# A conditioned decoder layer on one core: where the gate chunk's partial sums are added in the opening, and what orders the conditioning passes in the softmax

## The chip, the core and the metric

The kernel runs on one core of a Trainium2 chip. The core has a matrix engine (TensorE, PE in the profile, with its weight loads shown apart as PEld), a vector engine (VectorE, DVE), a scalar engine (ScalarE, ACT), a general engine (GpSimd, POOL) and an engine that mostly issues transfers (SyncE, SP). The metric is the device time of one execution in microseconds (us), as the median of several runs.

## What is computed

One layer: a SwiGLU feed-forward network, a mixing part with retention and windowed attention side by side, a second SwiGLU network, and a last norm. Scale, shift and gate of each part come from a product of a conditioning vector with a large matrix `w_ada`. Everything is float32. The core of it:

```python
c_act = jax.nn.silu(c)
mod = (c_act @ w_ada[l] + b_ada[l]).reshape(b, N_MOD, D_MODEL)
h = modulate(rms_norm(x, norm_ffn1[l]), mod[:, 0], mod[:, 1])
x = x + 0.5 * mod[:, 2][:, None, :] * swiglu(h, w_ffn1_gu[l], w_ffn1_down[l])
h = modulate(rms_norm(x, norm_mix[l]), mod[:, 3], mod[:, 4])
x = x + mod[:, 5][:, None, :] * token_mixing(h, w_in[l], ...)
h = modulate(rms_norm(x, norm_ffn2[l]), mod[:, 6], mod[:, 7])
x = x + 0.5 * mod[:, 8][:, None, :] * swiglu(h, w_ffn2_gu[l], w_ffn2_down[l])
```

with `swiglu(h) = (silu(gate) * up) @ w_down`, where gate and up are the two halves of `h @ w_gu`. There are 256 tokens (two halves of 128), the model width is 2048, the feed-forward width 5632.

## The kernel before

**Products.** Weights come from memory in pieces of 1 MB (four blocks of 128 rows by 512 columns) into one of four raw buffers (`load`, L365). `split` (L389, L391) makes two numbers of each weight: ACT casts it to a rounded `wh`, DVE subtracts to get the rest, `wl`. `products` (L374) then issues, for each block of rows, three products for each of the two token halves, so one split (two blocks) gives twelve matmuls of 512 columns. There are three pairs of `wh`/`wl` buffers. Sums stay in PSUM; the pool for them has four banks, and a chunk of 512 columns takes two, one for each token half.

**Who sets the order.** SP's instructions stay in the order in which the program writes them. The instructions of the other engines are ordered ahead of time by a list scheduler: each instruction may go as soon as its inputs and a buffer are free, and of those that may go the earliest in the program goes first. `tc.issue_after(x)` adds a rule that what is written inside comes behind `x` on the same engine. `low[-1]` is the latest subtraction for a `wl`, `cast[-1]` the latest cast. Some stages are ordered wholly by hand; the two that the change touches are not.

**The opening.** The first network's up product needs h, whose columns become ready as `w_ada` is worked through, so its first 16 chunks (eight pairs of a gate chunk, even, and an up chunk, odd) are computed in four groups of rows. After each group but the last, a chunk's sums are moved from the banks to `part_of(n)`, its parts in SBUF (`to_parts`). In the last group (rows 9 to 15, seven blocks, 42 matmuls a chunk) the chunks are visited in order 0 to 15. Nothing happens with the gate chunk's banks at the end of its own visit; after the up chunk's visit `swiglu_up` adds the parts to both (L720 for the gate, into a scratch tile of the pool `t512`, which has five; L721 for the up chunk, into the parts), applies Silu on ACT (L724), multiplies (L725) and hands the result on to be turned. After chunk 15 comes `ffn_up`, which computes the chunks that are left, whole.

**Conditioning.** `w_ada` is read row by row, a row being 2048 columns of 128 partitions (1 MB), and DVE multiplies and sums it with the conditioning vector in four passes of 512 columns (`ada_pass`, L222). From the opening's last group on this runs beside the products: `set_pace` starts a generator, `conditioning`, and `tick`, called after each set of products, advances it at a given rate, one pass a step. It asks for a row `pace["ahead"]` passes before the first use (L282, on SP). Each pass stands under `issue_after`: the first eight of a generator behind an operation handed to it, the others behind `low[-1]`.

In the mixing part the rows first lie in the raw buffers that the weights also use, two passes ahead; the rate is 0.95 of a pass for a set of products until the softmax starts, 0.25 (`RATE_SOFT`) during it, and 0.95 again after it (`RATE_AFTER`). Seven steps after that `rows_beside` moves the rows to a tile of their own, `rows_x`. The softmax runs in quads of heads beside the products: scores on PE (L1386), scale and mask (L1394), maxima (L1406), exponentials on ACT (L1415), scaling (L1422), split into planes on ACT (L1436), two transposes by transfer on SP (L1445), joining on DVE (L1457), and the product with the values (L1470).

Of the kernel before, what the change touches and what calls it, by code (L numbers as in the profile page):

```python
# [77 lines left out]
def layer_kernel(  # L78
# [23 lines left out]
    nc = tc.nc  # L102
# [106 lines left out]
    AQ = 4  # L209
# [7 lines left out]
    def ada_pass(k, w, sums, q, passes=AQ, first=0):  # L217

        n = D // passes
        at = slice(q * n, (q + 1) * n)  # L220
        here = w[:, (q - first) * n : (q + 1 - first) * n]
        nc.vector.tensor_tensor_reduce(  # L222
            out=here,
            in0=here,
            in1=cact[:, at],
            scale=1.0,
            scalar=0.0,
            op0=ALU.mult,
            op1=ALU.add,
            accum_out=sums[:, k, q : q + 1],  # L230
        )

    def ada_sums():
        return two.tile([P, KD, AQ], F32, tag="sums", name=nm("sums"))
# [33 lines left out]
    def conditioning(outputs, place, behind):  # L268


        tiles = [(m, k) for m, _, _ in outputs for k in range(KD)]
        held = {}
        step = asked = 0

        def ask(at):

            (m, k), q = tiles[at // AQ], at % AQ
            w = place()
            n = min(w.shape[1] * AQ // D, AQ - q)
            w = w[:, : n * D // AQ]  # L280
            c0 = q * D // AQ
            nc.sync.dma_start(  # L282
                w, w_ada[(m * KD + k) * P : (m * KD + k + 1) * P, c0 : c0 + n * D // AQ]
            )
            for i in range(n):
                held[at + i] = (w, q)
            return n

        for m, gain, row in outputs:
            sums = own_sums.pop() if own_sums else ada_sums()  # L290
            for k in range(KD):
                for q in range(AQ):
                    while asked <= step + pace["ahead"] and asked < AQ * len(tiles):
                        asked += ask(asked)
                    w, first = held.pop(step)
                    early_on = behind is not None and step < 2 * AQ
                    with tc.issue_after(behind.ins if early_on else low[-1]):
                        ada_pass(k, w, sums, q, first=first)
                    step += 1
                    if k == KD - 1 and q == AQ - 1:  # L300
                        ada_end(m, slice(0, KD), sums, gain)
                        if row is not None:
                            gate_out(m, row)
                    yield
# [16 lines left out]


    pace = {"steps": iter(()), "rate": 0.0, "due": 0.0, "behind": None}

    def set_pace(outputs, halves, place, ahead):
        assert next(pace["steps"], None) is None
        pace["steps"] = conditioning(outputs, place, pace["behind"])
        pace["rate"] = len(outputs) * KD * AQ / halves
        pace["due"] = 0.0
        pace["ahead"] = ahead  # L330
# [64 lines left out]
    cast, low, newest = [], [], []  # L395
# [314 lines left out]
    def swiglu_up(banks_g, banks_u, tiles, ci, parts=None, by_dma=False, behind=None):  # L710

        k0 = ci * KB
        dest = tiles[k0 // KD].rearrange("p (k s) -> p k s", s=S)
        kk = k0 % KD
        work = []
        for t in range(NT):
            s = t512()
            g, u = banks_g[t], banks_u[t]
            if parts is not None:
                nc.vector.tensor_add(s, g, parts[0][t])  # L720
                nc.vector.tensor_add(parts[1][t], u, parts[1][t])  # L721
                g, u = s, parts[1][t]
            with nullcontext() if behind is None else tc.issue_after(behind):
                nc.scalar.activation(s, g, AF.Silu)  # L724
            nc.vector.tensor_mul(s, s, u)  # L725
            if by_dma:
                work.append(turn_by_dma(dest[:, kk : kk + KB, t * P : (t + 1) * P], s))
                continue
            transpose_to(
                dest[:, kk : kk + KB, t * P : (t + 1) * P],  # L730
                lambda j: s[:, j * P : (j + 1) * P],
                KB,
            )
        if work:
            turns.append(later(work))
# [248 lines left out]
    behind = [[back.tile([P, CH], F32, tag="back", name=nm("back")) for _ in range(NT)] for _ in range(2)]  # L984

    def part_of(n):
        if n < 2:
            return behind[n]
        if n >= 14:
            return [beside[n - 14][:, t, :] for t in range(NT)]  # L990
        at = ((n - 2) % 4) * NT * CH
        return [part[(n - 2) // 4][:, at + t * CH : at + (t + 1) * CH] for t in range(NT)]
# [4 lines left out]
    def place(m, k):  # L997
        if k < 1:
            rows_of[m, k] = raw_row()
        else:  # L1000
            ring.reverse()
            rows_of[m, k] = ring[0]
        ada_load(m, k, rows_of[m, k], 2 if k < 2 else 1)
# [95 lines left out]
    banks, moved, unlinted, fresh, added = {}, set(), set(), set(), set()  # L1099
# [20 lines left out]
    with tc.manual_schedule(engines=ORDERED):  # L1120
# [14 lines left out]
        v, q = small(NT, "rvar"), small(NT, "rq2")  # L1135
# [118 lines left out]
    for g, ks in enumerate(groups):  # L1254
        final = g == len(groups) - 1
        by_vector = chunks[1::3] if g == 1 else ()
        if final:
            row_ring.append(two_rows(rows_home))
            set_pace(ROWS_FFN1, 192, place_row, 0)
        order = chunks if (len(groups) - g) % 2 else chunks[::-1]  # L1260
        coming = iter(()) if final else group(groups[g + 1], 1 if g == 0 else 2)
        due = 0 if final else 2 * len(groups[g + 1])
        stay = () if final else order[-2:]
        for i, n in enumerate(order):
            if g == 0 and n in firsts:
                continue
            visit(n, ks, n not in stay, final, final or (g == len(groups) - 2 and n in stay))
            if g:
                after = [(m, ks) for m in order[i + 1 : i + 2]]
                if not after and not final:  # L1270
                    after = [(n, groups[g + 1])]
                for m, ms in after:
                    ready(m, ms)
                    if m not in banks and not final:
                        open_banks(m, not (g == len(groups) - 2 and m in stay))
            if final:
                turn_step()
            last = len(order) - 2
            if g == 0:
                by = [min(due, -(-j * due // 12)) for j in (i - 2, i - 1)]  # L1280
                by = by[1] - by[0]
            else:
                by = (i + 1) * due // last - i * due // last if i < last else i == last
            for _ in range(by + (g == 0 and i == last)):
                next(coming, None)
            if g == 0:
                for m in {2: firsts[:1], 3: (order[2], firsts[1])}.get(i, order[i - 1 : i]):
                    if m not in stay:
                        to_parts(m)
                if i == 3:  # L1290
                    columns_rest()
                if i == 5:
                    roots_in_rows()
            if n in stay or g == 0:
                continue
            if not final:
                to_parts(n)
            elif n % 2:
                swiglu_up(
                    banks.pop(n - 1),  # L1300
                    banks.pop(n),
                    tiles,
                    n // 2,
                    (part_of(n - 1), part_of(n)),
                    n // 2 < 6,
                    cast[-1],
                )
# [15 lines left out]
    RATE_SOFT, RATE_AFTER = 0.25, 0.95  # L1323
    row_ring.clear()
    set_pace([(7, 2, None), (6, None, None), (5, None, 1.0)], 192 / 0.95, place_row, 2)

    def rows_beside():

        for _ in range(7):
            yield  # L1330
        row_ring.append(two_rows(one.tile([P, 2 * D], F32, tag="x", name="rows_x")))
        pace["ahead"] = 0

    def in_chunk(c0):
        return gemm(held, wi, [c0])[0]
# [9 lines left out]
    b = head  # L1345
# [14 lines left out]
    b = gemm(held, wi, [O_SV], ahead=ahead)[0]  # L1360
# [139 lines left out]
    for ci in range(4):  # L1500
        b = in_chunk(O_SQ + ci * CH)
        work = []
        for t in range(NT):
            u = t512()
# [14 lines left out]
    for a, off in ((0, O_RQ), (1, O_RK)):  # L1519
        for ci in range(2):  # L1520
            b = in_chunk(off + ci * CH)
            work = []
            for t in range(NT):
                u = t512()
# [71 lines left out]
    for ci in range(4):  # L1596
        b = in_chunk(O_RV + ci * CH)
# [14 lines left out]
    first = gates(0)  # L1612
# [3 lines left out]
    for ci in range(4):  # L1616
        b = in_chunk(O_RG + ci * CH)
        work = []
        for t in range(NT):
            u = t512()  # L1620
# [9 lines left out]
    for p in range(2):  # L1630
        sg = first if p == 0 else gates(p)
        c0s = [(2 * p + i) * CH for i in range(2)]
        for g, a, w in ((1, a_swa, w_swa_branch), (0, a_ret, w_ret_branch)):
            assert g == 1 or not turns
            banks = gemm(a, w[0], c0s)
# [150 lines left out]
```

## Time and profile before

| what | us |
|---|---|
| median of 3 runs | 2357.78 (2356.67 to 2358.15) |
| the profiled execution | 2356.72 |
| its span, first to last instruction | 2354.9 |
| PE busy | 2334.3 |
| DVE busy | 1684.4 |
| ACT busy | 1361.9 |
| the opening's last group | about 222 to 374.5 |
| the mixing part's products, as far as the softmax runs beside them | about 860 to 1105 |

The profiled execution is one of the program's executions; its trace is what the timeline, the waits and the chain are read from. A row of the timeline gives the start, the length, the engine, the line, the operation, output and inputs, the count of merged instructions and, in brackets, how long the engine was idle before and what ended that. A matmul is recorded with a modelled end, so consecutive ones overlap in the record; the time between starts is the better measure.

### The profile page before, as it was taken

How to read it: one execution, taken by the hardware profiler on the slowest of the kernel's cores; microseconds unless marked ns; L12 is line 12 of the kernel's file. 1: busy time of each engine (PE TensorE's matmuls, PEld its weight loads, DVE VectorE, ACT ScalarE, POOL GpSimd, SP SyncE). 2: the span in 40 equal slices, each digit the busy share in tenths (PEclk: the TensorE clock that was granted, in tenths of full speed). 3: DMA queues.
4: the chain of work that ended last, by engine and by line, in shares of the span. 5: the costliest groups of instructions: out<-in, count | busy, mean ns of one | idle time of the engine just before them, and what ended most of it. 6: DMA issues, size and time to landing. Idle time of an engine off the chain costs nothing.

```text
span 2354.9 us, 28573 instructions
## 1 busy us (share of the span) xinstructions
PE 2334.3 (99%) x10443; PEld 1917.9 (81%) x10443; DVE 1684.4 (72%) x2610; ACT 1361.9 (58%) x1889; POOL 19.9 (1%) x28
## 2 busy tenths in 40 slices
PE   8999999999999999999999999999999999999998
PEld 5888888888888887778888888888888888888887
DVE  7788887778877668876777876776555555555656
ACT  6776665455556567674556564466455454455544
POOL 0000000000000000000000000000000000000000
PEclk9999999999999999999999999999999999999999
DMA  9989999999875878877789888764777777776553
GB/s 367 341 344 390 312 326 345 307 294 321 285 269 217 275 265 243 243 216 268 282 266 312 286 301 284 276 223 177 236 243 249 248 239 259 242 240 201 193 197 125
DMA packets 205726, 630.37 MB, mean 268 GB/s; under 512 B 114641, under 2 KB 116433, under 8 KB 149265
## 3 DMA queue, kind: packets, MB, share of 16 engines
q1 hardware_dynamic: 203090, 617.54, 77.0%
q0 software_dynamic: 1600, 9.83, 1.1%
q8 instruction: 81, 1.33, 0.2%
q10 hardware_dynamic: 896, 1.19, 0.1%
q14 instruction: 59, 0.48, 0.1%
HBM read 598.60 MB, written 4.22 MB: 256 GB/s over the span
## 4 chain that ended last, share of the span: by engine, by line
PE 61%; DVE 1%; issue 0%; ACT 0%; DVEq 0%
PE pa L374 59%; PE ps L1470 0%; PE pd L1386 0%; PE ps L374 0%; DVE wl L391 0%; DVE soft L1457 0%; PE pd L1555 0%; PE pd L1568 0%; PE pd L1570 0%; PE pd L1569 0%; PE ps L1386 0%; PE ps L910 0%; DVE soft L1422 0%; PE pd L1558 0%; PE pd L910 0%
## 5 line engine op out<-in xcount | busy, mean ns | idle before, releaser
L391 DVE TENSOR_TENSOR wl<-raw,wh 128x1024 fp32r<-128x1024 f32 (+1 forms) x808 | 968.9, 1203 | 551.1 <-ACT wh L389 490.2
L389 ACT CAST wh<-raw 128x1024 fp32r<-128x1024 f32 (+1 forms) x808 | 833.1, 1037 | 829.5 <-PE pa L374 751.8
L374 PE MATMUL pa<-wh,hh 128*128 128x512 f32 x2184 | 598.1, 391 | 2.7 <-DVE a L721 1.3
L374 PE MATMUL pa<-wh,hl 128*128 128x512 f32 x2184 | 598.0, 390 | 0.0
L374 PE MATMUL pa<-wl,hh 128*128 128x512 f32 x2184 | 588.9, 389 | 0.9 <-DVE wl L391 0.9
L374 PEld LDWEIGHTS pa<-wh,hh 128*128 128x128 f32 x2184 | 407.6, 188 | 91.1 <-ACT wh L389 2.3
L374 PEld LDWEIGHTS pa<-wl,hh 128*128 128x128 f32 x2184 | 409.6, 188 | 87.5 <-DVE wl L391 1.8
L374 PEld LDWEIGHTS pa<-wh,hl 128*128 128x128 f32 x2184 | 409.7, 188 | 86.3 <-issue 0.8
L374 PE MATMUL pa<-wh,a 128*128 128x512 f32 x1824 | 452.1, 389 | 0.0
L374 PEld LDWEIGHTS pa<-wh,a 128*128 128x128 f32 x1824 | 341.6, 188 | 70.6
L222 DVE CUSTOM_DVE_ANT_0 slot<-slot,cact 128x512 f32<-128x512 f32 (+2 forms) x310 | 246.0, 803 | 6.0 <-DMA slot<-in_w_ada_dram 5.9
L374 PE MATMUL pa<-wl,a 128*128 128x512 f32 x912 | 245.1, 389 | 0.0
L374 PEld LDWEIGHTS pa<-wl,a 128*128 128x128 f32 x912 | 171.0, 188 | 35.4
L565 ACT COPY slot<-back 128x512 uint16<-128x512 uint16 x148 | 98.8, 767 | 0.0
L424 ACT CAST a<-slot 128x512 fp32r<-128x512 f32 x114 | 70.6, 620 | 32.8 <-PE pa L374 29.1
L222 DVE CUSTOM_DVE_ANT_0 rows_x<-rows_x,cact 128x512 f32<-128x512 f32 x124 | 84.9, 685 | 0.0
L425 DVE TENSOR_TENSOR a<-slot,a 128x512 fp32r<-128x512 f32 x114 | 78.1, 687 | 1.4 <-ACT a L424 1.2
L549 ACT COPY flat<-t 128x512 uint16<-128x512 uint16 x136 | 76.7, 618 | 2.6 <-DVE t L1543 1.6
L222 DVE CUSTOM_DVE_ANT_0 raw<-raw,cact 128x512 f32<-128x512 f32 (+1 forms) x72 | 51.0, 715 | 0.0
L1244 ACT COPY slot<-pa 128x512 f32<-128x512 f32 x64 | 34.7, 591 | 22.6 <-PE pa L374 22.5
L374 PE MATMUL pa<-wh,home 128*128 128x512 f32 x160 | 39.5, 389 | 0.0
L222 DVE DVE_READ_ACCUMULATOR2_ANT sums<- 128x1 f32 x442 | 36.7, 83 | 0.0
(234 smaller groups left out, 1090.4 us busy)
## 6 DMA issues: line engine op xcount, KB each, us to landing
raw<-in_w_ffn_gu_dram SPq DMA_DIRECT2D x144, 1024.0 KB, 5.7
raw<-in_w_in_dram SPq DMA_DIRECT2D x104, 1024.0 KB, 5.4
raw<-in_w_ffn_down_dram SPq DMA_DIRECT2D x88, 1024.0 KB, 5.1
slot<-in_w_ada_dram SPq DMA_DIRECT2D x132, 512.0 KB, 6.0
rows_x<-in_w_ada_dram SPq DMA_DIRECT2D x62, 512.0 KB, 6.0
slot<-in_w_ada_dram SPq DMA_DIRECT2D x28, 1024.0 KB, 7.3
raw<-in_w_ffn_gu_dram SPq DMA_DIRECT2D x32, 768.0 KB, 6.1
raw<-in_w_ada_dram SPq DMA_DIRECT2D x17, 1024.0 KB, 5.6
```

Of the source, the lines that this page charges most:

```text
L222: nc.vector.tensor_tensor_reduce(out=here, in0=here, in1=cact[:, at], scale=1.0, scalar=0.0, op0=ALU.mult, op1=ALU.add, accum_out=sums[:, ...
L374: product = nc.tensor.matmul(banks[t], act[:, j, t * P : (t + 1) * P], weights[:, j, :], start=starts and i == 0 and j == 0, stop=ends and ...
L389: cast.append(nc.scalar.copy(hi, src).ins)
L391: low.append(nc.vector.tensor_sub(lo, src, hi.bitcast(F32)).ins)
L424: nc.scalar.copy(hi, v)
L425: nc.vector.tensor_sub(lo, v, hi.bitcast(F32))
L549: nc.scalar.copy(planes[:, i, :], words(src)[:, :, i])
L565: nc.scalar.copy(into[:, :, :, i], held["turned"][:, i])
L1244: nc.scalar.copy(p, b)
```

## The change

In the opening's last group a gate chunk's sums are added to its parts, in place, at the end of its own visit, and `swiglu_up` then reads the gate from the parts. And a switch, `pace["one_by_one"]`, is on at first, is turned off as the mixing part's conditioning is set up, and on again when its rows move to `rows_x`; while it is off, passes after the first eight stand under no `issue_after`.

```diff
@@ conditioning
-                    early_on = behind is not None and step < 2 * AQ
-                    with tc.issue_after(behind.ins if early_on else low[-1]):
+                    first_ones = behind is not None and step < 2 * AQ
+                    if first_ones or pace["one_by_one"]:
+                        with tc.issue_after(behind.ins if first_ones else low[-1]):
+                            ada_pass(k, w, sums, q, first=first)
+                    else:
                         ada_pass(k, w, sums, q, first=first)
@@ beside the first pace
+    pace["one_by_one"] = True
@@ swiglu_up
             if parts is not None:
-                nc.vector.tensor_add(s, g, parts[0][t])
                 nc.vector.tensor_add(parts[1][t], u, parts[1][t])
-                g, u = s, parts[1][t]
+                g, u = parts[0][t], parts[1][t]
@@ the opening's loop over chunks
             if not final:
                 to_parts(n)
-            elif n % 2:
+            elif n % 2 == 0:
+                for p, b in zip(part_of(n), banks.pop(n)):
+                    nc.vector.tensor_add(p, b, p)
+            else:
                 swiglu_up(
-                    banks.pop(n - 1),
+                    (None, None),
                     banks.pop(n),
@@ behind the mixing part's set_pace
+    pace["one_by_one"] = False
@@ rows_beside
         row_ring.append(two_rows(one.tile([P, 2 * D], F32, tag="x", name="rows_x")))
         pace["ahead"] = 0
+        pace["one_by_one"] = True
```

## The prediction

> **What bounds the kernel now.** I read the page first, then who PE waited for, then PE's busy time by stretches, then the chain of waits, and last the timeline around each stretch in which PE stood still.
>
> ```profile
> span 2354.9 us, 28573 instructions
> PE 2334.3 (99%) x10443; PEld 1917.9 (81%) x10443; DVE 1684.4 (72%) x2610; ACT 1361.9 (58%) x1889; POOL 19.9 (1%) x28
> ...
> 1523.04 0.11 PE ps L309
> ...
> 1644.59 445.67 PE pa L374 x1966
> ```
>
> The first two rows are the page: PE is busy for 2334.3 of 2354.9 us, so all idle time together is 20.6 us. The others are pieces of the chain of waits (start, length, what, count). In the long piece 445.67 / 1966 = 0.2267 us pass from one 512-column matmul to the next, and nothing but PE is in the chain there. So where PE runs it runs at its pace, and an edit that removes no matmul can only win the time in which PE waits. Where that is:
>
> ```profile
> PE ps L1049 <- ACT t L1045: 3.8, 1, 3.8
> PE pa L177 <- DMA c_row<-in_c_dram: 2.7, 1, 2.7
> PE pa L1115 <- ACT t L642: 2.3, 2, 1.8
> PE pa L374 <- DVE a L721: 1.3, 1, 1.3
> PE pa L374 <- DVE wl L391: 0.9, 2, 0.8
> PE pa L374 <- ACT wh L389: 0.8, 2, 0.4
> ...
> 350.00:375.00 25.00, 24.52 (x113) 1.00 1.05 357
> 375.00:400.00 25.00, 24.15 (x111) 1.00 0.89 326
> ```
>
> The upper rows are PE's waits (total us, times, longest). The first three belong to the opening ahead of its last group, which the change doesn't touch. What the change can reach is the wait for L721 (1.3 us, once) and those for wl and wh in the softmax. The lower rows (stretch, length, PE busy and matmuls, clock, DMA share, GB/s) give the place of the first: PE loses 0.48 + 0.85 us on the two sides of 375.
>
> **Part one: the add in place.** It removes no instruction and adds none: a pair had two adds of its gate chunk (L720), two of its up chunk (L721), two Silu and two products, and it has them still, with the gate adds writing to the parts instead of to a scratch tile. What moves is when the gate chunk's two banks come free.
>
> ```profile
> 231.31 1.28 DVE L720 TENSOR_TENSOR t<-pa,back 128x512 f32<-128x512 f32 x2
> ...
> 241.52 1.29 DVE L721 TENSOR_TENSOR back<-pa,back 128x512 f32<-128x512 f32 x2
> ...
> 370.55 1.23 DVE L391 TENSOR_TENSOR wl<-raw,wh 128x1024 fp32r<-128x1024 f32 x1 [1.06 <-ACT wh L389]
> ...
> 374.25 0.27 PE L309 MATMUL ps<-small_c,modc 128*16 128x128 f32 x1
> ...
> 375.02 1.29 DVE L721 TENSOR_TENSOR a<-pa,a 128x512 f32<-128x512 f32 x2
> ...
> 375.85 0.70 PE L374 MATMUL pa<-wh,hh 128*128 128x512 f32 x2 [1.34 <-DVE a L721]
> ...
> 376.22 1.28 DVE L720 TENSOR_TENSOR t<-pa,a 128x512 f32<-128x512 f32 x2
> ...
> 377.42 1.22 DVE L391 TENSOR_TENSOR wl<-raw,wh 128x1024 fp32r<-128x1024 f32 x1
> ```
>
> These are timeline rows (start, length, engine, line; in brackets the idle time before and what ended it). In the first pair the scheduler has already put the gate adds a whole visit ahead of the up adds (231.31 against 241.52): there the edit changes nothing. Only in the last pair do they come behind the up adds (376.22 after 375.02), although DVE stood idle meanwhile, for 1.06 us ahead of 370.55; what they lacked was, I infer, a free scratch tile. So all four banks are full as the group ends, and PE waits until L721 has emptied one. PE's last instruction before the wait started at 374.25 and takes 0.11 by the chain's row of the same line, so the next matmul was due at 374.36 and came at 375.85: **1.49 us lost**, once. With the add in place the gate banks are empty most of a visit earlier, and a visit is 42 x 0.2267 = 9.5 us. What is late next: the next wl (377.42) is queued behind both pairs of adds, but with the gate adds (1.28 us) gone from there it starts that much earlier, nearly as much as PE does. I take the whole 1.49 as gained; the bounds are 0 (another order of DVE keeps a bank full) and 1.49. In the other pairs the add lies about where it lay, at no cost; in the last it falls into gaps like the one just named. The parts are now read by ACT's Silu instead of by L720, some us later. The first transposed output that is written over parts comes at 283.82, over 40 us after the first pair's adds, so nothing waits for that:
>
> ```profile
> 283.82 2.67 ACT L565 COPY slot<-back 128x512 uint16<-128x512 uint16 x4
> ```
>
> **Part two: free passes.** In the softmax a conditioning pass no longer has to follow the latest wl on DVE. Count and work stay: one pass is 0.686 us and a short read-out. Its row's load stays where SP's hand-written order has it. A pass can now only move forward, to any time after its row has landed. Two things follow: DVE has one operation less behind each wl, and the row's raw buffer, one of the four which the weights also use, comes free earlier.
>
> ```profile
> L222 DVE CUSTOM_DVE_ANT_0 raw<-raw,cact 128x512 f32<-128x512 f32 x68 | 46.1, 686 | 0.0
> ...
> 885.03 0.33 SPq L282 DMA_DIRECT2D raw<-in_w_ada_dram  x1
> ...
> 958.96 0.69 DVE L222 CUSTOM_DVE_ANT_0 raw<-raw,cact 128x512 f32<-128x512 f32 x1
> ...
> 959.69 0.33 SPq L365 DMA_DIRECT2D raw<-in_w_in_dram  x1
> ...
> ACT wh L389 <- DMA raw<-in_w_in_dram: 31.0, 7, 5.2
> ...
> 898.26 1.05 ACT L389 CAST wh<-raw 128x1024 fp32r<-128x1024 f32 x1 [5.14 <-DMA raw<-in_w_in_dram]
> ...
> 902.74 1.07 PE L374 MATMUL pa<-wl,hh 128*128 128x512 f32 x4
> ...
> 903.92 1.20 PE L374 MATMUL pa<-wh,hh 128*128 128x512 f32 x4
> ...
> 907.68 1.07 PE L374 MATMUL pa<-wl,hh 128*128 128x512 f32 x4
> 908.25 1.21 DVE L391 TENSOR_TENSOR wl<-raw,wh 128x1024 fp32r<-128x1024 f32 x1
> ...
> 909.51 1.20 PE L374 MATMUL pa<-wl,hh 128*128 128x512 f32 x4 [0.77 <-DVE wl L391]
> ...
> 984.28 1.07 PE L374 MATMUL pa<-wl,hh 128*128 128x512 f32 x4
> ...
> 985.52 1.20 PE L374 MATMUL pa<-wl,hh 128*128 128x512 f32 x4 [0.17 <-DVE wl L391]
> ```
>
> The row asked for at 885.03 keeps its buffer for 74 us, until its fourth pass, at 958.96 (counted off, four passes to a row); SP's next weight load starts as that pass ends, at 959.69. Meanwhile ACT waits for raw weights 7 times, 31.0 us in the stretch 840 to 1060, once for 5.14 us up to 898.26. That late cast is followed by the exponentials, so the next casts are late, and DVE behind them. What PE loses, by starts: due 902.74 + 4 x 0.2267 = 903.65, came 903.92: 0.27. Due 908.59, came 909.51: 0.92. Due 985.19, came 985.52: 0.33. Together **1.52 us**, more than the 1.05 of the waits' rows, since a matmul's recorded end lies past the time at which the next may start. A buffer holds two blocks of 12 matmuls, 24 x 0.2267 = 5.44 us of PE; weights one buffer further ahead cover even the longest wait of ACT, 5.14. The bounds from the first direction are 0 (SP's queue, not the buffer, delays the weights) and 1.52. I take the two linked stalls, 0.27 + 0.92 = 1.19, because the wait of 5.14 us stands right before them, and leave the third.
>
> The other direction is the cost. DVE works in the order it was given. A pass moved forward can lie ahead of a wl and hold it up for 0.69 us, or stand at DVE's head until its row lands.
>
> ```profile
> DVE slot L222 <- DMA slot<-in_w_ada_dram: 5.9, 7, 1.5
> ```
>
> This row of the waits has passes that stood for their row, in the FFN stages: 7 times, 1.5 us at most, 0.84 in the mean, and no wait of PE is put down to it. In the softmax wl has less lead: that of 908.25 ended 0.87 us after PE was due at 908.59, so there such a wait would reach PE in full.
>
> The Trainium skill (TensorE: Matmul & The Clock Gate, section on the 16 sub-arrays) calls VectorE's queue strict FIFO, while TensorE may pull weight loads forward. By that rule a pass that waits for its row holds back every wl behind it, and the sum would be that of the third rival below; the timeline rows above agree, in that the wl of 377.42 stands behind all four adds.
>
> **The sum.** The profiled execution took 2356.72 us, its span 2354.9 and 1.8 around it. 1.49 + 1.19 = 2.68 off gives 2354.0. The median of the three runs, 2357.78, lies 1.06 above that execution, so in its terms **2355.1 us**. The bounds of the gain are 0 and 1.49 + 1.52 = 3.01.
>
> **Rivals.** First: only the wait at 375 goes, and the softmax keeps its stalls because SP's queue holds the weights back.
>
> ```profile
> 886.74 5.81 SPq L1445 DMA_TRANSPOSE a<-planes_of  x2
> 892.64 14.07 SPq L365 DMA_DIRECT2D raw<-in_w_in_dram  x3
> ```
>
> For it: SP is taken up for 5.81 us by the two transposes of a quad, and the weights' load comes right after, at 892.64, whatever buffer is free. Against: with a buffer more that load would have been asked for ahead of the transposes. 2357.78 - 1.49 = 2356.3.
>
> Second: nothing goes; the change doesn't do what it says for time, because each wait is taken over by another at its place (a bank that L721 frees no sooner, a cast behind the exponentials). 2357.8. Against it: the gate banks have no other reader than the two adds.
>
> Third, the slower side: a pass at DVE's head waits for its row. In the stretch that the edit frees, eleven rows begin their loads, from 787.58 to 1086.88:
>
> ```profile
> 787.58 0.33 SPq L282 DMA_DIRECT2D raw<-in_w_ada_dram  x1
> ...
> 1086.88 0.33 SPq L282 DMA_DIRECT2D raw<-in_w_ada_dram  x1
> ```
>
> At the mean wait of 0.84 us, four of them (those under the quads, where wl has no lead) cost 3.4, and all eleven 9.3. With the gain of part one that is 2357.78 + 3.4 - 1.49 = 2359.7, or 2357.78 + 9.3 - 1.49 = 2365.6. It decides once the wait is longer than wl's lead over PE. For it speaks the slim lead; against it that the row is asked for two passes ahead, and that the passes from raw have 0.0 us of idle time before them now, although some come soon after their row.
>
> **How the numbers follow.** Forecast 2355.1: 0.53 (its own range, the run-to-run spread in it, 2353.7 to 2356.2). First rival 0.18. Second 0.10. Third at its lower price 0.11, at its higher 0.05. A gain over all bounds, by waits that I don't see: 0.03. What a measurement can tell from no change is about 0.2%, 4.7 us: faster means under 2353.1, slower over 2362.5. All the forecast and the first two rivals lie inside. So faster 0.03, same 0.91, slower 0.06. The range runs from 2357.78 - 3.01 - 1.1 (the lowest of the runs lies 1.1 under their median) = 2353.7 up to 2359.7, the third rival's lower price, rounded to 2359.8.
>
> **What would show it.** After the change: no PE wait for L721 or its successor at 375; the last pair's gate adds about 365; passes from raw in bunches soon after their row lands; fewer and shorter waits of ACT for the raw weights of w_in between 840 and 1060; no PE wait of 0.77 for wl. Wrong would be: idle time of DVE in front of L222 ended by the row's DMA, with a PE wait for wl behind it; wl of the last group held up by the moved adds; or new PE waits after 1100 us, where only the changed order of the scheduler could have brought them.

## The result, and the profile after

The changed kernel takes 2353.72 us in the median of 22 runs (2353.12 to 2354.92), the one before 2357.22 in 22 runs beside them (2356.52 to 2358.72). The ratio is 0.9985, with a 95% interval from 0.9979 to 0.9991: 3.50 us faster, and no run of one kernel lies among those of the other. The profiled execution has a span of 2351.9 us against 2354.9.

First PE's waits in the changed kernel (total us, times, longest). Its line numbers are a few higher: the products are L378, the subtraction for wl L395.

```profile
PE ps L1052 <- ACT t L1048: 4.2, 1, 4.2
PE pa L1118 <- ACT t L646: 3.0, 2, 1.8
PE pa L177 <- DMA c_row<-in_c_dram: 2.4, 1, 2.4
PE pa L378 <- ACT wh L393: 0.8, 2, 0.4
PE pa L378 <- ACT pa L1213: 0.5, 1, 0.5
```

The rows for L721 and for wl are gone; the one for wh is as it was. PE's busy time by stretches (length, busy, matmuls, clock, DMA share, GB/s) says where. The first two rows are of the kernel before, the other four of the changed one:

```profile
900.00:925.00 25.00, 24.13 (x119) 1.00 0.80 244
975.00:1000.00 25.00, 24.83 (x123) 1.00 0.78 222
...
350.00:375.00 25.00, 25.00 (x116) 1.00 1.04 347
375.00:400.00 25.00, 25.00 (x116) 1.00 0.94 356
900.00:925.00 25.00, 25.00 (x125) 1.00 0.89 229
975.00:1000.00 25.00, 25.00 (x125) 1.00 0.95 264
```

With the two rows ahead of 400 us that the prediction shows, each of the four stretches was short of PE work before and is full now. The timeline of the opening's end, after the change (L1303 is the gate's add in place, L724 the up chunk's):

```profile
365.85 1.28 DVE L1303 TENSOR_TENSOR a<-pa,a 128x512 f32<-128x512 f32 x2
...
374.75 0.27 PE L312 MATMUL ps<-small_c,modc 128*16 128x128 f32 x1
374.78 1.17 PE L378 MATMUL pa<-wh,hh 128*128 128x512 f32 x4
...
375.53 1.28 DVE L724 TENSOR_TENSOR a<-pa,a 128x512 f32<-128x512 f32 x2
```

The gate's add has gone from 376.22 to 365.85, into the visit of the up chunk, and the next group's first matmul starts 0.03 us after PE's previous instruction instead of 1.60 (375.85 - 374.25): **1.57 us won**. (The opening itself ran 0.5 us later in this execution than in the one profiled before; executions differ by that.)

For the softmax, the first scores, those of the second and third quad, and the last, before and after. Between the first and the last lies the same PE work:

```profile
864.91 1.14 PE L1386 MATMUL pd<-slot,slot 64*128 64x256 f32 x8
...
888.41 1.13 PE L1386 MATMUL pd<-slot,slot 64*128 64x256 f32 x8
...
913.37 1.13 PE L1386 MATMUL pd<-slot,slot 64*128 64x256 f32 x8
...
1039.73 1.14 PE L1386 MATMUL pd<-slot,slot 64*128 64x256 f32 x8
```

```profile
863.84 1.14 PE L1394 MATMUL pd<-slot,slot 64*128 64x256 f32 x8
...
887.33 1.13 PE L1394 MATMUL pd<-slot,slot 64*128 64x256 f32 x8
...
910.82 1.13 PE L1394 MATMUL pd<-slot,slot 64*128 64x256 f32 x8
...
1036.72 1.13 PE L1394 MATMUL pd<-slot,slot 64*128 64x256 f32 x8
```

174.82 us became 172.88: **1.94 us won**. It lies in two places: from the second to the third scores 24.96 us became 23.49 (1.47 won), and from the fifth to the sixth 25.65 (963.73 to 989.38 before) became 25.18 (0.47 won). From the matmul at 375 to the first scores it is 489.06 us before and after, and from the last scores to the end 1315.2, so nothing else moved that counts. The two sums give 1.57 + 1.94 = 3.51, the difference of the medians 3.50. That these agree to 0.01 is luck: the same pair of kernels, measured again below, differed by 3.00.

How the passes lie now, in the timeline after:

```profile
878.95 0.33 SPq L282 DMA_DIRECT2D raw<-in_w_ada_dram  x1
...
880.67 6.17 SPq L1453 DMA_TRANSPOSE a<-planes_of  x2
...
884.77 0.69 DVE L222 CUSTOM_DVE_ANT_0 raw<-raw,cact 128x512 f32<-128x512 f32 x1 [2.38 <-DMA raw<-in_w_ada_dram]
...
886.61 0.69 DVE L222 CUSTOM_DVE_ANT_0 raw<-raw,cact 128x512 f32<-128x512 f32 x1
...
886.94 3.00 SPq L369 DMA_DIRECT2D raw<-in_w_in_dram  x3
...
887.22 2.36 DVE L395 TENSOR_TENSOR wl<-raw,wh 128x1024 fp32r<-128x1024 f32 x2
...
890.79 1.07 PE L378 MATMUL pa<-wl,hh 128*128 128x512 f32 x4
```

The row asked for at 878.95 has had all four passes by 887.3; before, such a row kept its buffer for 74 us. DVE now stands 2.38 us at the head of its queue for that row. In the waits of the whole mixing part this is a row of its own:

```profile
DVE raw L222 <- DMA raw<-in_w_ada_dram: 14.7, 10, 4.6
```

Ten such waits, and PE is full through them (from 875 to 900 its busy time is 25.00). Three lie between the first and the last scores: 2.38 us at 884.77, 0.64 at 981.56 and 1.08 at 1033.36. The longest, 4.6, comes behind the softmax's quads, at 1123.10. ACT's waits for the raw weights of w_in between 840 and 1060, 31.0 us before, have no row left.

### The profile page after: what moved, and what is told of

Same layout as the page of the kernel before. It is cut to its first block, busy times and chain, and to the rows that moved or that the text cites. A ratio compares the mean times of both kernels' runs of the same rounds, so it can differ in the third digit from the quotient of the medians.

```text
span 2351.9 us, 28585 instructions
## 1 busy us (share of the span) xinstructions
PE 2332.9 (99%) x10443; PEld 1918.4 (82%) x10443; DVE 1684.6 (72%) x2610; ACT 1363.2 (58%) x1889; POOL 18.6 (1%) x28
## 3 DMA queue, kind: packets, MB, share of 16 engines
q10 hardware_dynamic: 896, 1.19, 0.1%
## 4 chain that ended last, share of the span: by engine, by line
PE 98%; DMA 1%; DVE 1%; ACT 0%; issue 0%; SPq 0%; DVEq 0%; ACTq 0%
PE pa L378 95%; PE ps L1478 0%; DMA slot<-in_w_ada_dram 0%; PE pd L1394 0%; DMA x_sb<-in_x_dram 0%; DVE slot L222 0%; PE ps L378 0%; PE ps L913 0%; PE ps L1394 0%; PE pd L1577 0%; PE pd L1578 0%; PE pd L1576 0%; PE pd L1563 0%; ACT slot L1247 0%; PE ps L536 0%
## 5 line engine op out<-in xcount | busy, mean ns | idle before, releaser
L395 DVE TENSOR_TENSOR wl<-raw,wh 128x1024 fp32r<-128x1024 f32 (+1 forms) x808 | 969.0, 1204 | 533.7 <-ACT wh L393 471.6
L378 PE MATMUL pa<-wh,hh 128*128 128x512 f32 x2184 | 597.5, 391 | 1.2 <-ACT wh L393 0.8
L378 PE MATMUL pa<-wh,hl 128*128 128x512 f32 x2184 | 597.3, 390 | 0.0
L378 PE MATMUL pa<-wl,hh 128*128 128x512 f32 x2184 | 588.1, 389 | 0.0
L378 PEld LDWEIGHTS pa<-wh,hh 128*128 128x128 f32 x2184 | 407.8, 188 | 89.0 <-issue 2.4
L378 PEld LDWEIGHTS pa<-wh,hl 128*128 128x128 f32 x2184 | 409.9, 188 | 85.8 <-issue 0.4
L378 PEld LDWEIGHTS pa<-wl,hh 128*128 128x128 f32 x2184 | 409.7, 188 | 85.9 <-issue 0.8
L378 PE MATMUL pa<-wh,a 128*128 128x512 f32 x1824 | 452.2, 389 | 0.0
L378 PEld LDWEIGHTS pa<-wh,a 128*128 128x128 f32 x1824 | 341.6, 188 | 70.6
L378 PE MATMUL pa<-wl,a 128*128 128x512 f32 x912 | 245.1, 389 | 0.0
L378 PEld LDWEIGHTS pa<-wl,a 128*128 128x128 f32 x912 | 171.1, 188 | 35.4
L429 DVE TENSOR_TENSOR a<-slot,a 128x512 fp32r<-128x512 f32 x114 | 78.1, 687 | 0.1
L378 PE MATMUL pa<-wh,home 128*128 128x512 f32 x160 | 39.5, 389 | 0.0
```

Of the source, the lines that this page charges most:

```text
L378: product = nc.tensor.matmul(banks[t], act[:, j, t * P : (t + 1) * P], weights[:, j, :], start=starts and i == 0 and j == 0, stop=ends and ...
L395: low.append(nc.vector.tensor_sub(lo, src, hi.bitcast(F32)).ins)
L429: nc.vector.tensor_sub(lo, v, hi.bitcast(F32))
```

## The experiments

Two questions were open: whether each part brings what the trace puts at its place, and why. For the softmax there were two theories. **Buffer**: a row's raw buffer comes free earlier, so that the weights run further ahead. **Order**: passes no longer stand between two subtractions for wl on DVE. For the opening: **scratch** (the gate's add came late in the last pair because it had no scratch tile) against **program order** (because it is written late).

All runs in a table; "scores" is the time from the first to the last scores, "raw wait" ACT's wait for raw weights of w_in between 840 and 1060 us, both from one profiled execution.

| kernel | median us | before, beside it | ratio (95% interval) | scores | raw wait |
|---|---|---|---|---|---|
| before | 2357.22 | | | 174.82 | 31.0 |
| changed | 2353.72 | 2357.22 | 0.9985 (0.9979 to 0.9991) | 172.88 | none |
| add alone | 2354.97 | 2356.69 | 0.9994 (0.9985 to 1.0002) | 174.03 | 27.1 |
| free passes alone | 2355.22 | 2356.69 | 0.9994 (0.9985 to 1.0003) | 172.89 | none |
| buffer held | 2355.88 | 2356.69 | 0.9997 (0.9988 to 1.0005) | 174.75 | 31.6 |
| in place, written late | 2354.88 | 2356.69 | 0.9992 (0.9983 to 1.0001) | 174.41 | 25.3 |
| changed, again | 2353.46 | 2356.46 | 0.9986 (0.9977 to 0.9995) | 172.89 | none |
| first pass held | 2353.53 | 2356.46 | 0.9987 (0.9978 to 0.9995) | 172.89 | 0.6 |
| copies only | 2353.44 | 2356.46 | 0.9986 (0.9977 to 0.9995) | 172.88 | none |
| free everywhere | 2367.0 | 2356.46 | 1.0044 (1.0031 to 1.0057) | 172.89 | none |

The first four trials below the changed kernel ran on one chip and the last four on another, each group beside its own runs of the kernel before. The intervals of the small effects reach 1, so there the traces decide, and the medians go with them.

### Each part alone

The add alone: the changed kernel without the line that turns the switch off.

```diff
-    pace["one_by_one"] = False
```

> The add in place alone; passes stay behind the latest wl. If the two parts add up, as the traces say (1.57 us by the place of the next group's first matmul, 1.94 us in the softmax), this gives 2357.2 - 1.6 = 2355.6 us, PE does not wait at 375 us, and the softmax keeps all its stalls (ACT waits about 31 us for the raw weights of w_in between 840 and 1060, PE waits 0.77 and 0.17 for wl). If the scheduler's new order after the opening had itself brought the softmax's gain, this alone would give about 2353.7.

The free passes alone: the changed kernel with the gate's add where it was.

```diff
-                g, u = parts[0][t], parts[1][t]
+                nc.vector.tensor_add(s, g, parts[0][t])
+                ...
+                g, u = s, parts[1][t]
@@
-            elif n % 2 == 0:
-                ...
+            elif n % 2:
+                swiglu_up(
+                    banks.pop(n - 1),
```

> The free passes alone; the gate chunk is added with its pair, through the scratch tile. If the parts add up: 2357.2 - 1.9 = 2355.3 us, PE waits 1.3 us for L721's successor at 375 as before, and no wait for wl in the softmax. If the softmax's gain hung on part one, 2357.2.

Measured: 1.72 us gained by the add alone, 1.47 by the free passes alone; together 3.19, against 3.50 and 3.00 in the two measurements of the changed kernel. PE's waits with the add alone and with the free passes alone:

```profile
PE pa L378 <- DVE wl L395: 0.8, 1, 0.8
```

```profile
PE pa L378 <- DVE a L725: 1.3, 1, 1.3
```

With the add alone the wait at 375 is gone and one of the softmax is there; with the free passes alone it is the other way round, and the scores take 172.89 us. So the parts are separate and add up. One expectation missed by a little: with the add alone the softmax lost 174.03 - 172.88 = 1.15 us, not 1.94. The constrained softmax has no fixed loss: with the add alone 1.12 of it lies between the second and third scores and only 0.03 between the fifth and sixth; with "in place, written late" it lost 1.53 in all. What sets it from case to case wasn't followed.

### Why the add came late

The kernel before, with one line changed: the add stays where it is written, with its pair, but goes in place.

```diff
-                nc.vector.tensor_add(s, g, parts[0][t])
+                nc.vector.tensor_add(parts[0][t], g, parts[0][t])
                 nc.vector.tensor_add(parts[1][t], u, parts[1][t])
-                g, u = s, parts[1][t]
+                g, u = parts[0][t], parts[1][t]
```

> The kernel before with the gate's add in place, but still written with its pair, after the up chunk's visit; passes as before. Scratch theory (in the last pair the gate's add came late because no scratch tile was free): the scheduler now moves the add forward by itself, PE does not wait at 375, 2355.6. Program-order theory (it came late because it is written late): the wait at 375 stays and the time is 2357.2.

Measured: 2354.88 us, as the add alone. The timeline:

```profile
366.07 0.69 DVE L720 TENSOR_TENSOR a<-pa,a 128x512 f32<-128x512 f32 x1
368.42 0.69 DVE L720 TENSOR_TENSOR a<-pa,a 128x512 f32<-128x512 f32 x1
...
374.97 0.27 PE L309 MATMUL ps<-small_c,modc 128*16 128x128 f32 x1
374.99 1.17 PE L374 MATMUL pa<-wh,hh 128*128 128x512 f32 x4
```

Written late, the add is still moved forward by the scheduler to 366, and PE goes on at once. Scratch holds, program order falls: of part one, writing in place alone does the work, and the new place in the program wasn't needed. A sixth scratch tile would be the more direct trial; it was not tried.

### Why the softmax has no stalls

The changed kernel, with a copy of one column inside the row's buffer at the old place of the fourth pass. It changes no result, since the row has been used; it only holds the buffer.

```diff
                     else:
                         ada_pass(k, w, sums, q, first=first)
+                        if q == AQ - 1:
+                            with tc.issue_after(low[-1]):
+                                nc.vector.tensor_copy(w[:, :1], w[:, 1:2])
```

> The changed kernel, passes free, but one copy of a single column in the row's raw buffer stands behind the latest wl at the old place of the row's fourth pass, so that the buffer is held as long as before. It adds 15 or so copies of under 0.1 us on DVE. Buffer theory (the gain comes from the raw buffer that weights get earlier): ACT waits for the raw weights again (20 to 31 us between 840 and 1060) and the softmax's 1.9 us are lost again, 2355.6. Order theory (the gain comes from passes no longer standing between two wl): 2353.7, the same as the changed kernel.

And the control, the same copies from a constant to itself:

```diff
-                                nc.vector.tensor_copy(w[:, :1], w[:, 1:2])
+                                nc.vector.tensor_copy(eps, eps)
```

> Control for the held buffer: the same small copies at the same places, but from a constant to itself, so that no raw buffer is held. Buffer theory: no stall of PE in the softmax, 172.9 us from the first to the last scores, time as the changed kernel, 3.5 us under the one before. If the copies themselves, or the order that they bring, cost the time: about 0.8 us under the one before, as with the held buffer.

With the buffer held the passes still run in bunches, but the scores take 174.75 us again and ACT starves again; rows of its timeline:

```profile
898.15 2.00 ACT L396 CAST wh<-raw 128x1024 fp32r<-128x1024 f32 x2 [4.93 <-DMA raw<-in_w_in_dram]
...
907.86 0.15 DVE L304 COPY raw<-raw 128x1 f32<-128x1 f32 x1
...
908.00 1.19 PE L381 MATMUL pa<-wl,hh 128*128 128x512 f32 x4 [0.38 <-DVE wl L398]
```

It is the chain of before once more: a wait of ACT of nearly 5 us, and some 10 us later PE stops for wl. The control, with 14 copies as well (147 ns in the median against 148), takes 172.88 us for the scores and 2353.44 in all, like the changed kernel. So neither the copies nor the order that they bring cost anything, and the held buffer costs 174.75 - 172.88 = 1.87 of the 1.94 us; behind the last scores it costs some 0.6 more (1315.8 us to the end against 1315.2). Buffer holds; order falls. The run times point the same way: with the buffer held they lie between 2353.88 and 2357.94, with the control between 2353.17 and 2353.81. Why the first scatter so widely stays open; starved weights alone don't do it, since the runs of the add alone, where ACT waits 27.1 us, lie between 2354.70 and 2355.81.

The last of this group holds only the first pass of a row at its old place.

```diff
-                    if first_ones or pace["one_by_one"]:
+                    if first_ones or pace["one_by_one"] or q == 0:
```

> The changed kernel, but the first pass of each row stays behind the latest wl at its old place and only the other three are free, so they follow it at once. The raw buffer is then held from its load to the first pass (some 25 us in the softmax) instead of to the fourth (74 us). Buffer theory: most of the 1.9 us stays won, time within 0.5 us of the changed kernel, since a buffer held for a third of the time starves the weights seldom; ACT's waits for raw w_in between 840 and 1060 lie between 0 and 31 us. Order theory (passes must leave their place between two wl): the first passes still stand there, so a quarter of the loss is back, 0.5 us.

It took 2353.53 us, no stall, ACT's raw wait 0.6 us. It agrees with buffer, since a buffer that is held for a part of the time is enough; taken by itself it tells little, as order's 0.5 us is near what a median scatters. The changed kernel beside it:

> The changed kernel itself once more, beside the runs below on one chip: 3.5 us under the kernel before. Its softmax should again take 172.9 us from the first to the last scores (863.84 to 1036.72 in its trace), with no wait of ACT for the raw weights of w_in there.

2353.46 us, 3.00 under the one before, within the interval of the first measurement.

### Free passes everywhere

```diff
     pace = {"steps": iter(()), "rate": 0.0, "due": 0.0, "behind": None}
-    pace["one_by_one"] = True
+    pace["one_by_one"] = False
@@ rows_beside
         pace["ahead"] = 0
-        pace["one_by_one"] = True
```

> Passes free everywhere after the first eight of a generator, in the FFN stages too, with the add in place. The changed kernel's trace has no wait of PE after the opening, so there is nothing left to win: the same time as the changed kernel within 0.5 us. The slower side: in the FFN stages rows are asked for with no pass of lead, so a pass may stand longer at the head of DVE's queue than wl leads PE; every wait of a microsecond that reaches PE would be seen as a wait for wl, and the time would be 1 to 5 us above the changed kernel.

2367.0 us, 10.5 above the kernel before and 13.5 above the changed one: the slower side, and more than was given for it. Waits of DVE, then of PE, then PE's busy time by stretches:

```profile
DVE slot L222 <- DMA slot<-in_w_ada_dram: 95.1, 78, 3.0
DVE rows_x L222 <- DMA rows_x<-in_w_ada_dram: 76.8, 53, 3.8
DVE raw L222 <- DMA raw<-in_w_ada_dram: 11.1, 6, 6.1
```

```profile
PE pa L378 <- DVE wl L395: 2.9, 6, 1.0
...
PE pa L378 <- DVE a L429: 1.7, 3, 0.9
PE pa L378 <- DVE t L662: 1.6, 2, 1.2
```

```profile
625.00:650.00 25.00, 22.91 (x97) 1.00 0.69 253
...
1275.00:1300.00 25.00, 23.50 (x101) 1.00 0.95 324
```

Outside the stretch that the change freed, passes now stand for their rows 78 + 53 times, 171.9 us in all (in the changed kernel 7 times, 7.1 us), and what is queued behind them on DVE (wl, the activations' low parts at L429, the gated sums at L662) comes late. In the changed kernel both stretches have 25.00 us of PE. The rows of PE's waits shown add up to 6.2 us only; as in the softmax, where 0.9 us in the row for wl stood for a loss of 1.94, they understate it. By the profiled executions 7.4 us are lost up to the first scores (871.26 against 863.84) and 5.9 behind the last. The number of waits doesn't set that price: from 1350 us on passes stand 56 times, 64.2 us in all, and up to 2300 no wait of PE is on record. That the waits cost the 13.5 us is read from these rows; no trial parts them from the other changes of order. The raw passes of the mixing part wait here too, 11.1 us, and the scores still take 172.89.

## Why the prediction was right or wrong

The forecast was 2355.1 us and the range 2353.7 to 2359.8; 2353.72 lies at its very edge. Of the 1.4 us between them 0.56 is the kernel before, which came out at 2357.22 in 22 runs instead of 2357.78 in three, and 0.82 the gain: sized at 2.68 us, measured at 3.50. The direction, both places and the mechanism of each part were right. Two steps failed. The term of part two was mis-sized: 1.19 us, and 1.94 measured. And the change was called too small to tell from none: by a bound of 0.2%, 4.7 us, 0.91 went to "the same", while 22 runs of each kernel settle the ratio to 0.0006 either way, 1.4 us, and the change is 3.50.

- **Part one** was given 1.49 us and brought 1.57. The missing 0.08 is PE's small instruction at 374.25, for which 0.11 us was set aside; after the change the next matmul starts 0.03 behind it. That a scratch tile was lacking was inferred, and the run with the add in place but written late bears it out.
- **Part two** was given 1.19 and brought 1.94. This is the term that was mis-sized, in two ways. The third stall (0.33 at 985.52) was put at nothing without a reason, and it went too. And each stall was priced by the matmul's late start alone. The four matmuls right behind a wait take longer as well: the row at 909.51 shows 1.20 us for four where others show 1.07, and the next row starts at 910.54, 1.03 later instead of 4 x 0.2267 = 0.91. That is 0.12 more for each of three stalls: 1.52 + 0.36 = 1.88, near the measured 1.94. Place by place the two linked stalls were given 1.19 and brought 1.47, the third was given 0 and brought 0.47. So the upper bound of 3.01 was no bound. A misreading cost nothing: PE's waits for wh (0.8 us, 2 times) were put into the softmax, but lie at 50.74 and 53.18 us, in the opening, and are there after the change too. The softmax's own stall for wh, at 903.92, stands in the row of the weight load alone, as 0.53 us.
- **The cause of part two**, a raw buffer more for the weights, held: shown by the held buffer and its control. (The buffer's "two blocks of 12 matmuls" are two splits; it holds four blocks.)
- **First rival**, SP's transposes hold the weights back: it fell. They still take SP 6.17 us at 880.67, and the load still comes after them, but earlier loads are further ahead.
- **Second rival**, the waits reappear at their places: it fell in both.
- **Third rival**, passes at DVE's head: the mechanism is there, and the price in this kernel is nothing. The row that it was priced from had waits of 1.5 us at most; there are ten here, in fourteen rows that are free instead of the eleven counted, with up to 2.4 us under the quads and 4.6 behind them. The step that failed in it is that such a wait "would reach PE in full" in the softmax. The lead of wl was taken from the moment of a stall; with weights in time the lead is longer. Of the 2.38 us at 884.77 nothing reached PE: the subtraction behind the passes began at 887.22, and the next product of a wl started at 890.79. With every pass free, 131 such waits went with 13.5 us more, but the 56 of them behind 1350 us with no wait of PE. That it is the lead which decides whether they cost is read from these rows, not tried by itself. The Trainium skill calls VectorE's queue strict FIFO (TensorE: Matmul & The Clock Gate, the section on the 16 sub-arrays); the trace agrees, since the casts for the wl of 887.22 were done by 885.5 and it still came behind all four passes.

## What to carry to other kernels

Where a side task borrows a buffer from the main stream, look at how long it keeps it, not only at what it computes: letting the borrower finish as soon as its data has landed can be worth more than spreading its work evenly. A late operation isn't always late by order; it may lack an output tile, and writing in place frees the scheduler to move it. The same freedom that helps with a few transfers costs with many: an instruction moved ahead of its data blocks all that is queued behind it, so set the length of its waits against the lead of what follows; their number alone doesn't give the price.

## What the runs showed of the hardware

After a wait PE loses more than the wait: the four matmuls behind it took about 0.12 us longer from start to start (1.03 against 0.91). The records of weight loads fit that: at 909.51 the weight load and the matmul start together, whereas in the running stream the load starts 0.23 us ahead of its matmul. It isn't the wait as such: the first four products behind the scores show the same 1.03 (866.42 to 867.45), and there too load and matmul start together, with no wait on record.

```profile
866.42 0.76 PEld L374 LDWEIGHTS pa<-wh,hh 128*128 128x128 f32 x4
866.42 1.19 PE L374 MATMUL pa<-wh,hh 128*128 128x512 f32 x4
867.45 1.08 PE L374 MATMUL pa<-wh,hl 128*128 128x512 f32 x4
...
907.45 0.87 PEld L374 LDWEIGHTS pa<-wl,hh 128*128 128x128 f32 x4
907.68 1.07 PE L374 MATMUL pa<-wl,hh 128*128 128x512 f32 x4
...
909.51 0.76 PEld L374 LDWEIGHTS pa<-wl,hh 128*128 128x128 f32 x4 [1.19 <-DVE wl L391]
...
910.54 1.08 PE L374 MATMUL pa<-wh,hh 128*128 128x512 f32 x4
```

These are rows of the kernel before. That the load is the cause was not tried by itself.
